# Two adjacent weight rows per partition, and the small start-up vectors on two queues, in a one-core encoder block with 32 experts

## The chip, the core and the metric

The kernel runs on one core of one Trainium2 chip. The core has five engines that run their own instruction streams: TensorE (PE; its weight loads are shown apart as PEld), VectorE (DVE), ScalarE (ACT), GpSimd (POOL) and SyncE (SP). Data comes from the chip's main memory by DMA, on 16 DMA engines that work for the core. A DMA is issued by an instruction of SP's or ACT's stream, in the order of that stream; in the profile such issues stand under SPq and ACTq, and the packets of SP's queue under q1, those of ACT's under q10.

The metric is the device time of one execution in microseconds (us). Before the change it is 1523.5 us, the median of 3 runs (1523.36 to 1524.43). The execution that was profiled took 1525.76 us, and the span of its trace, from the first to the last instruction, is 1524.1 us.

## The reference, cut to what matters

One layer over 256 tokens of width 1024: a mixer (attention and a state-space scan), a cross-attention, and a mixture of experts. The experts are where the changed loads feed in:

```python
logits = (xt @ w_router) + b_router                  # 256 tokens, 32 experts
top_vals, top_idx = lax.top_k(logits, TOP_K)         # 4 of 32
probs = jax.nn.softmax(top_vals, axis=-1)
...
def expert_block(args):
    xb, e = args
    g = jnp.minimum(xb @ w_e_gate[e] + b_e_gate[e], SWIGLU_LIMIT)
    u = jnp.clip(xb @ w_e_up[e] + b_e_up[e], -SWIGLU_LIMIT, SWIGLU_LIMIT)
    act = (u + 1.0) * g * jax.nn.sigmoid(SWIGLU_ALPHA * g)
    return act @ w_e_down[e] + b_e_down[e]
```

Each expert has three float32 matrices of 1024 x 1024 (4 MB each). All 32 experts are run, so 384 MB of weights pass through the core. The five vectors that change queue are the gain and bias of the first layer norm (`ln_in_g`, `ln_in_b`) and three of the scan: `dt_bias` and `a_log` (32 numbers each, for a softplus and a decay) and `d_skip` (32 numbers, one per scan head, that scale a skip path).

## The kernel before, in words

**Start.** The input `x` is fetched on SP's queue in four pieces, then `ln_in_g` and `ln_in_b` into rows of the tile `rows_a`, then the first five entries of a plan of weight blocks (`W.preload(5)`, L82: the first 1 MB in two halves, then two of 1 MB), then the other small vectors in rows (L225). The input is normalised (L270), transposed on TensorE (L278), scaled by the layer norm's gain and bias on ScalarE (L284), and split on VectorE into two parts `hTh` and `hTl` (L48, L49). Every weight block is also split into `w_h` (ScalarE, L96) and `w_l` (VectorE, L97), and a projection is three products (L237, L239, L240). Blocks come into three buffers `w_raw`; a scheduler orders each engine's stream by its own estimate of times.

**The scan's vectors.** `d_skip` is laid out by two DMAs (L392) as `dcol`: 64 partitions each read the same 16 numbers with a step of two. `dt_bias` and `a_log` follow on the same queue (L394, L395) into the two columns of `dtb`, one number per partition. ScalarE makes `nega` from `a_log` (L397), and VectorE changes its sign (L398).

**The mixture of experts.** A ring of 21 buffers `mw` of 1 MB takes the expert matrices in chunks of 256 rows (`fetch`, L662): partition p of a chunk holds row p and row 128 + p. A buffer is filled again when TensorE has read it. The plan takes the experts in pairs: gate and up of both (16 chunks), then down of both (8 chunks). Four experts make a quad; at its start `gather` (L961) selects each expert's at most 64 tokens with a product of the normalised input `xh`, `xl` (the weight load) and a selection matrix, and scales the result by `ln2_g` and `ln2_b` per feature (L966, L968). A chunk is used by 8 recorded matmuls (L935): the activations are loaded as weights, and the chunk streams by. Between up and down the activations are transposed (L948). `scatter` (L981) adds the results to the tokens. Experts with more than 64 tokens have a loop of their own (L1064 on) with its own loads (L1101); the trace shows no load of it. The down matrix of the last expert comes in pieces of 256 columns (L659), so that the first half of the output can be finished early.

Of the kernel before, what the change touches and what calls it, by code (L numbers as in the profile page):

```python
# [6 lines left out]
F32 = mybir.dt.float32  # L7
# [111 lines left out]
def body(nc, tc, a, out, dbg=None, stop=99):  # L119
# [7 lines left out]
    with es:  # L127
# [30 lines left out]
        for key, rows in (("a", ROWS_A), ("b", ROWS_B)):  # L158
            rowt[key] = (cst if key == "a" else xt_p).tile([P, P], F32, name="rows_" + key)
            n = 0  # L160
            for name, k in rows:
                if name.startswith("ln_in"):
                    nc.sync.dma_start(rowt[key][n:n + k], flat(name))
                else:
                    rest.append((rowt[key][n:n + k], flat(name)))
                at[name] = (key, n)
                n += k

# [51 lines left out]
                plan_block(a["w_xo"][0], "xo", 512 * i)  # L220

        plan_all()
        W.preload(5)
        for t, v in rest[::-1]:
            nc.sync.dma_start(t, v)  # L225

        def proj_t(name, c0, kts, xh, xl, r0=0):
# [141 lines left out]
        with tc.tile_pool(name="st", bufs=1, reuse_waits="tile") as st_p:  # L369
# [16 lines left out]
            nc.gpsimd.memset(past, 0.0)  # L386
            nc.gpsimd.affine_select(past, past, pattern=[[1, P]], compare_op=ALU.is_ge, fill=NEG, base=0,
                                    channel_multiplier=-1)
            dcol = xt_p.tile([P, 16], F32, name="dcol")
            dsv = a["d_skip"][0].rearrange("(c t) -> t c", t=2)  # L390
            for t in range(2):
                nc.sync.dma_start(dcol[64 * t:64 * t + 64], dsv[t:t + 1].broadcast_to([64, 16]))  # L392
            dtb = xt_p.tile([32, 2], F32, name="dtb")
            nc.sync.dma_start(dtb[:, 0:1], a["dt_bias"][0].rearrange("(p o) -> p o", o=1))  # L394
            nc.sync.dma_start(dtb[:, 1:2], a["a_log"][0].rearrange("(p o) -> p o", o=1))  # L395
            nega = xt_p.tile([32, 1], F32, name="nega")
            nc.scalar.activation(nega, dtb[:, 1:2], AF.Exp)  # L397
            nc.vector.tensor_scalar(nega, nega, -1.0, None, op0=ALU.mult)  # L398
# [247 lines left out]
        def fetch(upto):  # L646

            if not looped[0]:
                upto = min(upto, len(plan) // 2 + nslots - 4)
            while len(got) < min(upto, len(plan)):  # L650
                w, e, c = plan[len(got)]
                t = slot()
                if w == 2 and e == NE - 1:

                    t = t.rearrange("p j (k i f) -> p (j k) i f", k=2, i=2)
                    v = wes[w][e].rearrange("(c k p) (j i f) -> c p k j i f", c=2, p=P, j=2, i=2)[c % 2, :, :, :, c // 2]
                    for k in (slice(0, 2), slice(2, 4)) if c == 3 else (slice(0, 4),):
                        for i in range(2):
                            nc.sync.dma_start(t[:, k, i], v[:, k, i])  # L659
                    got.append(t)  # L660
                    continue
                ins = nc.sync.dma_start(t, wes[w][e, 256 * c:256 * c + 256].rearrange("(k p) f -> p k f", p=P))  # L662
                if len(ring) < nslots:
                    tc.keep_in_program_order(ins)
                got.append(t)
# [50 lines left out]
        nc.gpsimd.iota(iop_i, pattern=[[0, 1]], base=0, channel_multiplier=1)  # L716
        iop = cst.tile([P, 1], F32, name="iop")
        nc.gpsimd.tensor_copy(iop, iop_i)
        oneb = cst.tile([P, 1], BF16, name="oneb")
        nc.gpsimd.memset(oneb, 1.0)  # L720
        upb = cst.tile([P, P], BF16, name="upb")
# [217 lines left out]
        def swiglu(pg, gt, ut, st):  # L939
# [3 lines left out]
            nc.vector.scalar_tensor_tensor(ut, ut, 1.0, gt, op0=ALU.add, op1=ALU.mult)  # L943
            nc.vector.tensor_tensor(ut, ut, st, op=ALU.mult)

        def act_t(ut, pa, aT):
            for f in range(4):
                nc.tensor.transpose(pa[:, P * f:P * f + P], ut[:, P * f:P * f + P], ident)  # L948
            nc.scalar.activation(aT, pa.rearrange("p (f i c) -> p f i c", f=4, i=2), AF.Copy)  # L949

        def gather(sel, xg, n, ps, kts=(0, KT)):

            w = 512 // n
            for kt in range(*kts, w):
                p = ps()
                for i in range(w):
                    o = p[:, n * i:n * i + n]
                    for x in (xh, xl):
                        for b in range(NB):
                            s = slice(P * (kt + i), P * (kt + i) + P)  # L960
                            nc.tensor.matmul(o, x[:, b, s], sel[:, b], start=i == 0 and b == 0 and x is xh,  # L961
                                             stop=b == NB - 1 and x is xl, skip_group_check=True)
                for i in range(w):
                    o, g, b_ = p[:, n * i:n * i + n], col("ln2_g", kt + i), col("ln2_b", kt + i)
# [73 lines left out]
        def overflow():  # L1038
# [25 lines left out]
            with tc.If(nv > 0), tc.For_i(0, nv, 1):  # L1064
# [29 lines left out]
                for w in range(3):  # L1094
# [3 lines left out]
                    for c in range(4):  # L1098
                        wt = wb[n % 3]
                        n += 1  # L1100
                        nc.sync.dma_start(wt, wes[w][bass.ds(ev, 1), 256 * c:256 * c + 256].rearrange(  # L1101
                            "o (k p) f -> p (o k) f", p=P))
# [239 lines left out]
```

## Time and profile before

| | |
|---|---|
| median of 3 runs | 1523.5 us |
| the profiled execution | 1525.76 us |
| its span | 1524.1 us |
| PE busy | 1397.0 us (92%) |
| DVE, ACT busy | 635.6 us (42%), 415.7 us (27%) |
| moved by DMA | 489.69 MB, mean 321 GB/s |
| granted TensorE clock | 0.978 of full speed |

Busy time of PE has to be read with care: matmuls overlap, their ends are modelled, and a matmul that waits for its data inside the pipeline looks busy. The slices of the span tell more than the shares: the DMA engines are about half busy in the first third of the span and full from a bit past it to the end.

### The profile page before, as it was taken

Reading aid. Unit: us, or ns where it says so; the run is one execution under the profiler, and the core shown is the slowest. Engines: PE = TensorE matmul, PEld = TensorE weight load, DVE = VectorE, ACT = ScalarE, POOL = GpSimd, SP = SyncE. Lnnn points to the kernel's source line nnn. Section 1 sums busy time; section 2 is a strip of 40 time slices with the busy share of each in tenths; the row PEclk is TensorE's granted clock in tenths of the full one; section 3 lists DMA queues with packets and bytes.
Section 4 is the critical chain, followed back from the end, with each engine's and each line's share of the span. In section 5 each row is a group of like instructions: output and inputs, shape, how many; then the busy total and the mean of one; then the engine's idle time right before and its main releaser. Section 6 shows DMA issues by size and latency. Waiting matters only on the chain. (4 is left out here: it accounts for less than half of the span.)

```text
span 1524.1 us, 19108 instructions
## 1 busy us (share of the span) xinstructions
PE 1397.0 (92%) x7884; PEld 800.6 (53%) x7884; DVE 635.6 (42%) x1001; ACT 415.7 (27%) x656; POOL 19.2 (1%) x36
## 2 busy tenths in 40 slices
PE   2899999999999999989999999979889899888996
PEld 2898899998999863333333333324224233223233
DVE  3756568889877652441222121222112212212123
ACT  2557578687555411010010010001001001001010
POOL 1000000000000010000000000000000000000001
PEclk8899999999999999999999999989999999999999
DMA  3654536454595789999999999999999999999996
GB/s 113 183 169 162 181 124 209 152 194 139 192 327 173 252 302 398 409 409 404 409 409 409 409 409 409 409 409 355 409 409 409 409 410 409 409 409 408 409 409 235
DMA packets 154109, 489.69 MB, mean 321 GB/s; under 512 B 12396, under 2 KB 16996, under 8 KB 154020
## 3 DMA queue, kind: packets, MB, share of 16 engines
q1 hardware_dynamic: 153876, 488.18, 83.8%
q8 instruction: 63, 1.03, 0.3%
q10 hardware_dynamic: 144, 0.26, 0.0%
q14 instruction: 26, 0.21, 0.0%
HBM read 487.33 MB, written 1.08 MB: 320 GB/s over the span
## 5 line engine op out<-in xcount | busy, mean ns | idle before, releaser
L935 PE MATMUL ps_gu<-mw,xg 128*64 128x512 f32 x2048 | 465.8, 596 | 6.2 <-DMA mw<-in_w_e_up 3.8
L935 PEld LDWEIGHTS ps_gu<-mw,xg 128*64 128x64 f32 x2048 | 145.8, 137 | 280.4 <-issue 250.2
L935 PE MATMUL ps_y<-mw,aT 128*64 128x512 f32 x992 | 228.8, 599 | 14.7 <-DMA mw<-in_w_e_down 14.7
L97 DVE TENSOR_TENSOR w_l<-w_raw,w_h 128x1024 fp32r<-128x1024 f32 x145 | 175.8, 1217 | 90.1 <-ACT w_h L96 89.0
L96 ACT ACTIVATE w_h<-w_raw 128x1024 fp32r<-128x1024 f32 x145 | 152.6, 1055 | 122.7 <-PE ps_t L239 72.6
L239 PE MATMUL ps_t<-hTl,w_h 128*128 128x256 f32 x576 | 165.4, 288 | 21.4 <-DVE hTl L49 21.4
L237 PE MATMUL ps_t<-hTh,w_h 128*128 128x256 f32 x576 | 165.2, 288 | 2.0 <-DVE gx L327 2.0
L240 PE MATMUL ps_t<-hTh,w_l 128*128 128x256 f32 x576 | 164.0, 287 | 0.0
L935 PEld LDWEIGHTS ps_y<-mw,aT 128*64 128x64 f32 x992 | 70.9, 137 | 155.3 <-issue 124.3
L239 PEld LDWEIGHTS ps_t<-hTl,w_h 128*128 128x128 f32 x576 | 110.9, 193 | 21.8 <-DVE hTl L49 21.6
L237 PEld LDWEIGHTS ps_t<-hTh,w_h 128*128 128x128 f32 x576 | 110.8, 193 | 2.8 <-issue 2.8
L240 PEld LDWEIGHTS ps_t<-hTh,w_l 128*128 128x128 f32 x576 | 110.2, 192 | 0.4 <-issue 0.4
L942 DVE TENSOR_SCALAR ut<-ps_gu 128x512 f32<-128x512 f32 x32 | 22.1, 692 | 207.3 <-PE ps_gu L935 207.2
L949 ACT ACTIVATE aT<-ps_x 128x512 f32<-128x512 f32 x32 | 19.1, 597 | 314.5 <-PE ps_x L948 314.5
L889 PE MATMUL ps_gu<-bgu,ident 128*64 128x512 f32 x256 | 70.7, 619 | 28.4 <-DVE ut L942 13.5
L976 DVE SCALAR_TENSOR_TENSOR y<-ps_y,scl,y 128x512 fp32r<-128x512 f32 x30 | 22.5, 751 | 173.5 <-ACT y L975 167.6
L940 DVE TENSOR_SCALAR gt<-ps_gu 128x512 f32<-128x512 f32 x32 | 22.1, 691 | 159.3 <-PE ps_gu L935 159.3
L975 ACT ACTIVATE y<-ps_y,scl 128x512 fp32r<-128x512 f32 x30 | 19.0, 684 | 242.1 <-PE ps_y L935 197.5
L941 ACT ACTIVATE st<-gt 128x512 f32<-128x512 f32 x32 | 20.1, 629 | 198.2 <-DVE gt L940 198.2
L889 PEld LDWEIGHTS ps_gu<-bgu,ident 128*64 128x64 f32 x256 | 16.9, 138 | 72.2 <-DVE ut L942 29.4
L983 DVE TENSOR_TENSOR h<-h,ps_x 128x512 f32<-128x512 f32 x60 | 38.8, 682 | 15.2 <-PE ps_x L982 15.2
L968 ACT ACTIVATE xg<-ps_x,cols_a 128x256 f32<-128x256 f32 x32 | 18.1, 565 | 94.4 <-PE ps_x L961 94.4
(348 smaller groups left out, 1793.4 us busy)
## 6 DMA issues: line engine op xcount, KB each, us to landing
mw<-in_w_e_gate SPq DMA_DIRECT2D x128, 1024.0 KB
mw<-in_w_e_up SPq DMA_DIRECT2D x128, 1024.0 KB
mw<-in_w_e_down SPq DMA_DIRECT2D x124, 1024.0 KB
w_raw<-in_w_in SPq DMA_DIRECT2D x39, 1024.0 KB
w_raw<-in_w_ssd SPq DMA_DIRECT2D x8, 1024.0 KB
w_raw<-in_w_sb SPq DMA_DIRECT2D x4, 1024.0 KB
csb<-csd SPq DMA_DIRECT2D x8, 512.0 KB
w_raw<-in_w_mix_out SPq DMA_DIRECT2D x4, 1024.0 KB
```

The lines of the kernel that those rows point to most:

```text
L96: nc.scalar.activation(h, src, AF.Copy)
L97: nc.vector.tensor_tensor(l, src, h.bitcast(F32), op=ALU.subtract)
L237: nc.tensor.matmul(o, wh[:, k, s], xh[:, kt], start=first and j % 2 == 0, stop=False, skip_group_check=True)
L239: nc.tensor.matmul(o, wh[:, k, s], xl[:, kt], start=False, stop=False, skip_group_check=True)
L240: nc.tensor.matmul(o, wl[:, k, s], xh[:, kt], start=False, stop=last, skip_group_check=True)
L889: nc.tensor.matmul(pg[w][64 * i:64 * i + 64], hot4(2 * w + i), bgu, start=True, stop=False, skip_group_check=True)
L935: nc.tensor.matmul(dst[i], lhs(2 * c + k), chunk[:, k, 512 * i:512 * i + 512], start=first and c == 0 and k == 0, stop=c == 3 and k == 1, ...
L940: nc.vector.tensor_scalar(gt, pg[0], LIMIT, None, op0=ALU.min)
L941: nc.scalar.activation(st, gt, AF.Sigmoid, scale=1.702)
L942: nc.vector.tensor_scalar(ut, pg[1], -LIMIT, LIMIT, op0=ALU.max, op1=ALU.min)
L976: nc.vector.scalar_tensor_tensor(yl[r], y2[i][r], scl[r, i:i + 1], yh[r].bitcast(F32), op0=ALU.mult, op1=ALU.subtract)
L983: nc.vector.tensor_tensor(h2[:, b, s], h2[:, b, s], ps, op=ALU.add)
```

## The change

Two things change. First, partition p of an expert's chunk takes rows 2p and 2p + 1 of the 256 instead of rows p and 128 + p. The two are adjacent in memory, so each partition reads one run of 8 KB instead of two runs of 4 KB. What TensorE contracts must follow: feature 256 c + 2p + k now stands in partition p of slice k. So `gather` and the transposes of the activations read their columns with a step of two (`pairs`), and the per-feature scale and bias of `gather` come from a small table `gb2` in that order. The last expert's down matrix is cut in 16 pieces of 256 KB instead of 10 pieces.

Second, `ln_in_g`, `ln_in_b`, `dt_bias`, `a_log` and `d_skip` are issued from ScalarE's stream, ahead of its first computation; `d_skip` comes as one row of 32 numbers and is spread over the partitions by a matmul with a row of minus ones. The other vectors stay on SP's queue behind the first weights.

```diff
-                if name.startswith("ln_in"):
-                    nc.sync.dma_start(rowt[key][n:n + k], flat(name))
-                else:
-                    rest.append((rowt[key][n:n + k], flat(name)))
+                rest.append((rowt[key][n:n + k], flat(name)))
...
+        dtb = xt_p.tile([32, 2], F32, name="dtb")
+        drow = xt_p.tile([1, NHEAD], F32, name="drow")
+        for t, v in (*rest[:2], (dtb[:, 0:1], a["dt_bias"][0].rearrange("(p o) -> p o", o=1)),
+                     (dtb[:, 1:2], a["a_log"][0].rearrange("(p o) -> p o", o=1)),
+                     (drow, a["d_skip"][0].rearrange("(o e) -> o e", o=1))):
+            nc.scalar.dma_start(t, v)
         W.preload(5)
-        for t, v in rest[::-1]:
+        for t, v in rest[:1:-1]:
             nc.sync.dma_start(t, v)
...
+            ps = px.tile([P, 512], F32, tag="x", name="ps_ds")
+            nc.tensor.matmul(ps[:, :NHEAD], nones[0:1], drow, start=True, stop=True)
             for t in range(2):
-                nc.sync.dma_start(dcol[64 * t:64 * t + 64], dsv[t:t + 1].broadcast_to([64, 16]))
...
+                r = slice(64 * t, 64 * t + 64)
+                nc.vector.tensor_scalar(dcol[r], ps[r, t:NHEAD:2], -1.0, None, op0=ALU.mult)
...
-                    for k in (slice(0, 2), slice(2, 4)) if c == 3 else (slice(0, 4),):
+                    for g in range(2):
                         for i in range(2):
-                            nc.sync.dma_start(t[:, k, i], v[:, k, i])
+                            nc.sync.dma_start(t[:, 2 * g:2 * g + 2, i], v[g, :, :, i])
...
-                ins = nc.sync.dma_start(t, wes[w][e, 256 * c:256 * c + 256].rearrange("(k p) f -> p k f", p=P))
+                ins = nc.sync.dma_start(t, wes[w][e, 256 * c:256 * c + 256].rearrange("(p k) f -> p k f", p=P))
...
+        rows2 = xt_p.tile([8, 256], F32, name="rows2")
+        for j, n in enumerate(("ln2_g", "ln2_b")):
+            nc.sync.dma_start(rows2[4 * j:4 * j + 4], a[n][0].rearrange("(c f) -> c f", f=256))
+        gb2 = cst.tile([P, 2, 8], F32, name="gb2")
+        ps = px.tile([P, 512], F32, tag="x", name="ps_gb2")
+        for k in range(2):
+            nc.tensor.transpose(ps[:, 8 * k:8 * k + 8], rows2[:, k:256:2], ident[:8, :8])
+        nc.vector.tensor_copy(gb2, ps[:, :16].rearrange("p (k j) -> p k j", k=2))
...
+        def pairs(kt):
+
+            return slice(256 * (kt // 2) + kt % 2, 256 * (kt // 2) + 256, 2)
+
         def act_t(ut, pa, aT):
             for f in range(4):
-                nc.tensor.transpose(pa[:, P * f:P * f + P], ut[:, P * f:P * f + P], ident)
+                nc.tensor.transpose(pa[:, P * f:P * f + P], ut[:, pairs(f)], ident)
...
-                            s = slice(P * (kt + i), P * (kt + i) + P)
-                            nc.tensor.matmul(o, x[:, b, s], sel[:, b], start=i == 0 and b == 0 and x is xh,
+                            nc.tensor.matmul(o, x[:, b, pairs(kt + i)], sel[:, b], start=i == 0 and b == 0 and x is xh,
```

The order of the instructions moves at three places that matter below. At the start of ScalarE's stream, before the change (`w_h` is the rounded half of a weight block, `ln_t` the scaled input, `nega` the decay made from `a_log`):

```order
L133 ACT_TABLE_LOAD
L96 ACTIVATE w_h<-w_raw 128x1024 x2
L284 ACTIVATE ln_t<-ps_tr,cols_a 128x256 x4
L96 ACTIVATE w_h<-w_raw 128x1024 x2
L284 ACTIVATE ln_t<-ps_tr,cols_a 128x256 x4
L397 ACTIVATE nega<-dtb 32x1
L96 ACTIVATE w_h<-w_raw 128x1024 x3
```

And with the change:

```order
L133 ACT_TABLE_LOAD
L226 DMA rows_a<-in_ln_in_g 8x128
L226 DMA rows_a<-in_ln_in_b 8x128
L226 DMA dtb<-in_dt_bias 32x1
L226 DMA dtb<-in_a_log 32x1
L226 DMA drow<-in_d_skip 1x32
L401 ACTIVATE nega<-dtb 32x1
L96 ACTIVATE w_h<-w_raw 128x1024 x2
L288 ACTIVATE ln_t<-ps_tr,cols_a 128x256 x4
```

The five issues and `nega` now stand ahead of ScalarE's first weight split, where `nega` stood behind four splits and eight scalings.

On SP's queue behind the small rows, before the change (`bgu` holds the experts' biases, `wr` the router's weights, `w_raw 128x8x32` the columns of the projection for dt):

```order
L225 DMA rows_a<-in_ln_g 8x128
L392 DMA dcol<-in_d_skip 64x16x1 x2
L394 DMA dtb<-in_dt_bias 32x1
L395 DMA dtb<-in_a_log 32x1
L82 DMA w_raw<-in_w_in 128x4x512
L706 DMA bgu<-in_b_e_gate 32x512 x2
L706 DMA bgu<-in_b_e_up 32x512 x2
L73 DMA w_raw<-in_w_in 128x8x32
L709 DMA wr<-in_w_router 128x8x32
L82 DMA w_raw<-in_w_in 128x4x512 x7
```

And with the change:

```order
L229 DMA rows_a<-in_ln_g 8x128
L82 DMA w_raw<-in_w_in 128x4x512
L712 DMA bgu<-in_b_e_gate 32x512 x2
L712 DMA bgu<-in_b_e_up 32x512 x2
L715 DMA wr<-in_w_router 128x8x32
L728 DMA rows_4645<-in_ln_g 4x256
L728 DMA rows_4645<-in_ln_b 4x256
L73 DMA w_raw<-in_w_in 128x8x32
L82 DMA w_raw<-in_w_in 128x4x512 x7
```

The four DMAs of `dcol` and `dtb` are gone from between the small rows and the sixth weight DMA; `wr` and the two rows for `gb2` go ahead of the dt columns.

Where the expert chunks are issued in rows, at the start of the mixture of experts on SP's queue, before the change:

```order
L662 DMA mw<-in_w_e_gate 128x2x1024 x4
L662 DMA mw<-in_w_e_up 128x2x1024 x4
L662 DMA mw<-in_w_e_down 128x2x1024 x5
L1150 DMA bdn<-in_b_e_down 32x512 x2
L662 DMA mw<-in_w_e_down 128x2x1024 x3
```

And with the change:

```order
L668 DMA mw<-in_w_e_gate 128x2048 x4
L668 DMA mw<-in_w_e_up 128x2048 x4
L668 DMA mw<-in_w_e_down 128x2048 x5
L1169 DMA bdn<-in_b_e_down 32x512 x2
L668 DMA mw<-in_w_e_down 128x2048 x3
```

The number and the order of the chunks stay; each is now one run of 2048 numbers per partition instead of two of 1024.

## Rows read from the trace of the kernel before

**Rows 1.** The profile page: the span, and in 40 equal slices of it the busy share of the DMA engines in tenths and what they moved.

```profile
span 1524.1 us, 19108 instructions
...
DMA  3654536454595789999999999999999999999996
GB/s 113 183 169 162 181 124 209 152 194 139 192 327 173 252 302 398 409 409 404 409 409 409 409 409 409 409 409 355 409 409 409 409 410 409 409 409 408 409 409 235
```

**Rows 2.** Busy time in stretches of the mixture of experts. Columns: the stretch in us from the span's start, its length, busy us (and instructions) of PE, PEld, DVE, ACT, POOL, then the granted TensorE clock, the busy share of the DMA engines, and GB/s.

```profile
600.00:640.00 40.00, 40.00 (x186) 14.20 (x184) 10.33 (x27) 0.95 (x2) 0.00 (x0) 1.00 1.03 409
1040.00:1080.00 40.00, 38.76 (x188) 14.27 (x184) 7.71 (x14) 2.45 (x4) 0.00 (x0) 1.00 0.91 356
564.00:1494.00 930.00, 856.59 (x3970) 312.38 (x3970) 224.97 (x409) 79.36 (x131) 0.00 (x0) 0.99 1.02 405
```

**Rows 3.** Who waited for whom over the whole span: total us, times, longest. The rows in which TensorE or its weight load waits for an expert's down matrix.

```profile
PEld ps_y L935 <- DMA mw<-in_w_e_down: 28.9, 22, 2.4
PE ps_y L935 <- DMA mw<-in_w_e_down: 14.7, 20, 3.3
```

**Rows 4.** The chain of work that ended last, in order of time: start, us, what. Its first and its last stretch of DMA.

```profile
1066.95 19.05 DMA mw<-in_w_e_down
...
1448.06 18.46 DMA mw<-in_w_e_up
```

**Rows 5.** TensorE's instructions in order of time at the start of five quads (quads 0, 1, 2, 6 and 7), where the gather begins: start, us, what.

```profile
558.63 0.70 PE L961 MATMUL ps_x<-sel,xh 128*128 128x256 f32 x2
...
681.39 0.51 PE L961 MATMUL ps_x<-sel,xh 128*128 128x256 f32 x2 [0.25 <-DVE h L983]
...
793.12 0.79 PE L961 MATMUL ps_x<-sel,xh 128*128 128x256 f32 x2
...
1267.26 0.79 PE L961 MATMUL ps_x<-sel,xh 128*128 128x256 f32 x2
...
1391.22 0.50 PE L961 MATMUL ps_x<-sel,xh 128*128 128x256 f32 x2 [0.26 <-DVE h L983]
```

**Rows 6.** DMA by size: from the page the packets of the whole span and the issues of the gate matrices (count, KB each); then two stretches, columns as in rows 2, in which the queue is full of runs of 2 KB (`w_raw`, 512 columns) and of 1 KB (the last expert's pieces of 256 columns).

```profile
DMA packets 154109, 489.69 MB, mean 321 GB/s; under 512 B 12396, under 2 KB 16996, under 8 KB 154020
...
mw<-in_w_e_gate SPq DMA_DIRECT2D x128, 1024.0 KB
...
12.00:13.50 1.50, 0.24 (x1) 0.25 (x2) 1.36 (x3) 1.50 (x4) 0.00 (x0) 1.00 1.06 392
1498.00:1503.00 5.00, 5.00 (x26) 1.78 (x26) 0.00 (x0) 0.00 (x0) 0.00 (x0) 1.00 1.10 349
```

**Rows 7.** SP's DMA issues from 17 to 40 us: start, us until the last of them was issued, what.

```profile
17.75 1.43 SPq L392 DMA_DIRECT2D dcol<-in_d_skip  x2
19.23 3.11 SPq L394 DMA_DIRECT2D dtb<-in_dt_bias  x1
22.38 0.42 SPq L395 DMA_DIRECT2D dtb<-in_a_log  x1
22.92 0.39 SPq L82 DMA_DIRECT2D w_raw<-in_w_in  x1
```

**Rows 8.** Instructions in order of time at 42 us, with the idle time of the engine before them and what ended it.

```profile
41.96 0.20 ACT L397 ACTIVATE nega<-dtb 32x1 f32<-32x1 f32 x1 [24.12 <-DMA dtb<-in_a_log]
...
42.26 1.27 DVE L49 TENSOR_TENSOR hTl<-ln_t,hTh 128x512 fp32r<-128x512 f32 x2
...
42.99 0.58 PE L239 MATMUL ps_t<-hTl,w_h 128*128 128x256 f32 x1 [21.43 <-DVE hTl L49]
```

**Rows 9.** Busy time in stretches around that wait, columns as in rows 2.

```profile
22.00:24.00 2.00, 0.00 (x0) 0.00 (x0) 0.00 (x0) 0.00 (x0) 0.00 (x0) 1.00 0.05 0
30.00:32.00 2.00, 0.00 (x0) 0.00 (x0) 0.00 (x0) 0.00 (x0) 0.00 (x0) 0.50 0.05 0
43.00:46.50 3.50, 3.50 (x16) 3.50 (x17) 2.80 (x3) 1.06 (x2) 0.00 (x0) 0.50 0.64 119
46.50:50.00 3.50, 3.50 (x30) 3.50 (x29) 1.22 (x1) 1.12 (x2) 0.00 (x0) 0.93 0.87 280
```

**Rows 10.** The first ten microseconds, in order of time, as in rows 7 and 8; the last row is the one DMA that ScalarE's queue issues before the change (x count: least, median and most ns).

```profile
0.80 1.28 ACT L133 ACT_TABLE_LOAD   x1 [0.80 <-PEq L1331]
...
3.08 0.28 SPq L163 DMA_DIRECT2D rows_a<-in_ln_in_b  x1
...
7.25 0.26 PE L173 MATMUL ps_prm<-ident,rows_a 16*128 16x16 f32 x1 [7.25 <-DMA rows_a<-in_ln_in_b]
...
8.11 1.70 DVE L270 TENSOR_SCALAR h<-h,ln_mv,ln_rs 128x1024 f32<-128x1024 f32 x2
...
9.87 1.06 ACT L96 ACTIVATE w_h<-w_raw 128x1024 fp32r<-128x1024 f32 x1 [7.79 <-DMA w_raw<-in_w_in]
...
L1302 ACTq DMA_DIRECT2D out<-h x1: 372/372/372, 1519.5 to 1519.5; - x1
```

**Rows 11.** Instructions grouped by line, shapes kept apart: count, busy us, mean ns of one, and idle time before them. The gather's matmul and weight load, and the weight load of the activations' transposes.

```profile
L961 PE MATMUL ps_x<-sel,xh 128*128 128x256 f32 x128 | 30.6, 323 | 0.7 <-DVE h L983 0.7
L961 PEld LDWEIGHTS ps_x<-sel,xh 128*128 128x128 f32 x128 | 21.7, 209 | 18.6 <-DVE xg L966 8.9 <-issue 5.7 <-DVE h L983 3.9
L948 PEld LDWEIGHTS ps_x<-ident,ut 128*128 128x128 f32 x128 | 13.4, 140 | 30.2 <-issue 20.3 <-DVE ut L944 8.3 <-DVE gt L940 1.6
```

**Rows 12.** SP's issues of the last expert's down matrix: start, us until the last was issued, count.

```profile
1481.19 21.62 SPq L659 DMA_DIRECT2D mw<-in_w_e_down  x10
```

More of the change, by code (lines that the diff above doesn't have):

```diff
@@ L389, in body @@
             dcol = xt_p.tile([P, 16], F32, name="dcol")
-            dsv = a["d_skip"][0].rearrange("(c t) -> t c", t=2)
+            ps = px.tile([P, 512], F32, tag="x", name="ps_ds")
+            nc.tensor.matmul(ps[:, :NHEAD], nones[0:1], drow, start=True, stop=True)
             for t in range(2):
-                nc.sync.dma_start(dcol[64 * t:64 * t + 64], dsv[t:t + 1].broadcast_to([64, 16]))
-            dtb = xt_p.tile([32, 2], F32, name="dtb")
-            nc.sync.dma_start(dtb[:, 0:1], a["dt_bias"][0].rearrange("(p o) -> p o", o=1))
-            nc.sync.dma_start(dtb[:, 1:2], a["a_log"][0].rearrange("(p o) -> p o", o=1))
+                r = slice(64 * t, 64 * t + 64)
+                nc.vector.tensor_scalar(dcol[r], ps[r, t:NHEAD:2], -1.0, None, op0=ALU.mult)
             nega = xt_p.tile([32, 1], F32, name="nega")
@@ L655, in fetch @@
                     t = t.rearrange("p j (k i f) -> p (j k) i f", k=2, i=2)
-                    v = wes[w][e].rearrange("(c k p) (j i f) -> c p k j i f", c=2, p=P, j=2, i=2)[c % 2, :, :, :, c // 2]
-                    for k in (slice(0, 2), slice(2, 4)) if c == 3 else (slice(0, 4),):
+                    v = wes[w][e].rearrange("(c g p k) (j i f) -> c g p k j i f", c=2, g=2, p=P, j=2,
+                                            i=2)[c % 2, :, :, :, :, c // 2]
+                    for g in range(2):
                         for i in range(2):
-                            nc.sync.dma_start(t[:, k, i], v[:, k, i])
+                            nc.sync.dma_start(t[:, 2 * g:2 * g + 2, i], v[g, :, :, i])
                     got.append(t)
                     continue
-                ins = nc.sync.dma_start(t, wes[w][e, 256 * c:256 * c + 256].rearrange("(k p) f -> p k f", p=P))
+                ins = nc.sync.dma_start(t, wes[w][e, 256 * c:256 * c + 256].rearrange("(p k) f -> p k f", p=P))
                 if len(ring) < nslots:
@@ L959, in gather @@
                         for b in range(NB):
-                            s = slice(P * (kt + i), P * (kt + i) + P)
-                            nc.tensor.matmul(o, x[:, b, s], sel[:, b], start=i == 0 and b == 0 and x is xh,
+                            nc.tensor.matmul(o, x[:, b, pairs(kt + i)], sel[:, b], start=i == 0 and b == 0 and x is xh,
                                              stop=b == NB - 1 and x is xl, skip_group_check=True)
                 for i in range(w):
-                    o, g, b_ = p[:, n * i:n * i + n], col("ln2_g", kt + i), col("ln2_b", kt + i)
+                    o, g, b_ = p[:, n * i:n * i + n], *[gb2[:, (kt + i) % 2, 4 * j + (kt + i) // 2:4 * j + (kt + i) // 2 + 1]
+                                                        for j in range(2)]
                     if i % 2:
@@ L1101, in overflow @@
                         nc.sync.dma_start(wt, wes[w][bass.ds(ev, 1), 256 * c:256 * c + 256].rearrange(
-                            "o (k p) f -> p (o k) f", p=P))
+                            "o (p k) f -> p (o k) f", p=P))
                         lhs = (lambda kt: aT[:, kt % 4, kt // 4]) if w == 2 else (lambda kt: xg[:, kt, 0:CAP])
```

## The prediction, made before the change was run

> **What bounds the kernel now.** I read the slices of the page first. From the sixteenth slice on the DMA engines are full and move 409 GB/s; before that they are about half busy [rows 1]. So the span has two parts with different limits. In the first, some 560 us, TensorE's products set the pace; in the second, the experts' 384 MB.
>
> The table of stretches says how firm the second limit is: 409 GB/s at a share of 1.03 from 600 to 640 us, and 405 GB/s on the mean of the 930 us from 564 to 1494, one dip to 356 included [rows 2]. TensorE looks busy there too, but a matmul that waits inside the pipeline looks busy. The waits name the down matrices as what its weight loads wait for, 28.9 us in 22 waits, beside 14.7 us of its matmuls [rows 3], and in the chain of what ended last stretches of DMA begin at 1066.95 us and the last of 18.46 us begins at 1448.06 [rows 4]. The starts of the quads show why only from there: quad 1 lasts 793.12 - 681.39 = 111.7 us with a full ring behind it, quad 6 lasts 1391.22 - 1267.26 = 124.0 us [rows 5]. A quad's 48 chunks of 1.0486 MB need 123.1 us at 409 GB/s. TensorE alone is 11 us quicker per quad than the loads, uses up the ring's stock by about 1060 us, and then runs at the pace of the loads.
>
> The first part has one large hole. At 21.6 us TensorE stops for 21.4 us: it waits for `hTl`, VectorE's `hTl` stands behind the sign change of `nega`, and ScalarE's `nega` stands 24.1 us until `a_log` has landed [rows 8]. `a_log` was issued at 22.38, behind the two DMAs of `dcol` and that of `dt_bias` [rows 7]. In the hole the DMA engines are 0.05 busy and move nothing that shows [rows 9]: 0.05 is a little under one engine of 16. The two `dcol` DMAs ask for 2 x 64 x 16 = 2048 numbers of 4 bytes; some 20 us for them would be about 10 ns each on one engine (an estimate from these rows).
>
> **The change, part by part.** The sum is made against the profiled execution: 1525.8 us, a span of 1524.1 and 1.7 around it, 2.3 us above the median.
>
> *The start.* `dcol`'s DMAs are gone, and `dt_bias` and `a_log` are issued some 19 us earlier on another queue. The hole of 21.4 us goes: -21.4. With it goes a slow restart: from 43 to 46.5 us the granted clock is 0.50 (1.2 GHz, after the idle time) and 16 matmuls start, in the next 3.5 us 30 do [rows 9]; the 16 would have taken 16/30 of 3.5 us = 1.9, so -1.6.
>
> What could be late next are the weights. When TensorE reached 21.6 us it had used two of the six half-blocks of the first 3 MB. Four are left, of 24 matmuls each at 3.5/30 = 0.117 us [rows 9]: 11 us, to about 33 us. The next weight DMA was issued at 22.92 [rows 7]; with four DMAs gone from ahead of it, it can go at about 17.75. Its 1.05 MB take 2.7 us at 392 GB/s [rows 6], and a small DMA behind loads took 4.2 us to arrive (issued 3.08, used 7.25) [rows 10]: in hand by about 25 us, 8 us early.
>
> What the new order adds is a wait ahead of everything on ScalarE and VectorE: `nega` now stands before ScalarE's first weight split (9.87 us) and its sign change before VectorE's normalisation (8.11 us) [rows 10]; behind them queue the splits, `hTh`, `hTl` and TensorE. ScalarE is done with its table load at 2.08; an issue on its queue took 0.37 us [rows 10], so `a_log`, the fourth, is issued at about 3.6 and, with the same 4.2 us, is there at 7.8: cost 0 to 0.3 us. If the issue of `dt_bias` takes 3.11 us as on SP's queue [rows 7], it is 2.7 us later. The far end is that `a_log` arrives only after all of `x` and the first weights, about 14.5 us: 6.4 us late. I take +1.0, the nearest row being that of `ln_in_b`; in it are the few small additions to TensorE and VectorE (the product that spreads `d_skip`, two small transposes, three copies), each like the 0.26 us transpose of rows 10. Start: -22.0, from -16 to -23. Everything behind shifts with it, since the ring and the stream start when the first part ends.
>
> *The stream.* Each partition's two runs of 4 KB become one of 8 KB. No load of 8 KB runs is in the trace, so it is bounded by the shorter ones. With the queue full the rates are 349 GB/s for 1 KB, 392 for 2 KB, 409 for 4 KB [rows 2, 6]; per engine (16 of them) that is 46.9, 83.6 and 160.2 ns a run. A fixed part and a part per KB, through 1 and 4 KB: 9.2 + 37.8 per KB, so 8 KB take 311.4 ns, 421 GB/s. Through 2 and 4 KB: 7.0 + 38.3, 313.4 ns, 418 GB/s. I take 419, by the nearer pair. The lower end is no gain (runs cut at 4 KB on the way, or 409 a limit of something else), the upper one no fixed part at all, 16 x 1024/37.8 = 433 GB/s. The stretch of 930 us moved 405 x 930 = 376.7 MB [rows 2]: 921 us at 409, 899 at 419, so -22.
>
> The Trainium skill, DMA: Bandwidth & Descriptors, section Why small descriptors are slow (HBM only), gives a fixed overhead of about 3 cycles per packet of 32-byte beats. By it 8 KB would save 3 beats in some 260, 1.2% or about 11 us, and the sum would be near 1491; but from 2 to 4 KB it would give 2.3%, where rows 6 and 2 show 4.3%.
>
> Can TensorE follow? At 419 a quad's load takes 120.1 us, still over its own 111.7, so the loads stay what ends last from about quad 1 on. In quad 0 TensorE itself needs 681.39 - 558.63 = 122.8 us [rows 5]; the ring is full there and a faster load waits for free buffers, so the 2.7 us of that quad are not had. Stream: -19. If loads cost nothing, TensorE's own 111.7 us would bring quad 7 to 681.4 + 6 x 111.7 = 1351.6, against 1391.2: some 40 us is the most.
>
> *Columns with a step of two.* The gather's and the transposes' weight loads now read every second number. A quad has 32 + 16 of them (256 and 128 in 8 quads [rows 11]). No weight load with a step is in the trace. From below they cost 0; from above, the whole 0.209 us of a gather's load once more [rows 11], 10 us a quad. I take 0: that load runs beside a matmul of 0.323 us, and TensorE has 8 us a quad to spare. Without that cover it is the third rival.
>
> *The end.* The last expert's matrix has 16 issues instead of 10, 6 x 0.3 us more on SP, inside 21.6 us in which SP waits for buffers [rows 12]: 0. The runs there stay 1 KB.
>
> Sum: 1525.8 - 21.4 - 1.6 + 1.0 - 19 = 1484.8 for an execution like the profiled one; less 2.3, **1482** as a median.
>
> **The rivals.** *The rate stays 409.* For it: 409 holds to a unit in nearly every slice, as a ceiling would. Against it: the steps from 1 to 2 to 4 KB have not flattened to nothing. Then only the start counts: 1525.8 - 22 - 2.3 = 1501.5.
>
> *The vectors come no sooner.* `a_log` shares the DMA engines with 1 MB of `x` and 3 MB of weights, lands near 14.5 us, and holds ScalarE and VectorE from the start. 6.4 us late instead of 1.0: 1488. Against it: `ln_in_b`, behind all of `x` on one queue, was there at 7.25 [rows 10]. The Trainium skill, same page, section Issuing engines are not separate DMA queues, says that a second issuing engine saves issue time only, since all run on the same DMA engines; that speaks for this rival.
>
> *Slower: the stepped weight loads are paid in full.* TensorE then needs 121.7 us a quad and becomes the limit. Quad 0 starts at 536.6 and takes 132.8, six quads 730.2, so quad 7 starts at 1399.6; from there to the end the span before took 132.9 with about 12 of waits, now 131: 1530.5, +1.7 - 2.3 = 1530, slower by 0.4%. It decides from 0.19 us per load: with x us a quad, 536.6 + 122.8 + 6 x 111.7 + 120.9 + 8x reaches 1524.1 at x = 9.2. For it: 48 such loads a quad sit on the engine that is next in line. Against it: they run beside matmuls.
>
> *Both ends good.* No fixed part per run, 433 GB/s: 118 us a quad even so, 921 - 870 = -51 cut by TensorE's 40 us: 1525.8 - 22 - 40 - 2.3 = 1461.
>
> **How the numbers follow.** Forecast 0.62; rate unchanged 0.18; vectors no sooner 0.08; both ends good 0.07; slower 0.05. The forecast alone, with 414 to 424 GB/s and the start's bounds, spans 1473 to 1495. Rival one and a start of -20 set the upper end at 1504; the lower one, 1467, takes in part of the last rival. About 0.2% (3 us) is what a measurement here can tell from no change. Every case but the third rival lies over 15 us below 1523.5; a milder form of it gives no change. Faster 0.93, same 0.02, slower 0.05.
>
> **What would show it.** The hole at 21 to 43 us gone and TensorE running through with the granted clock at 1.00; `nega` near 8 us; the first quad's gather near 537 us; packets of 8 KB, half as many, and slices of about 419 GB/s; quads of 120 us late and 112 early; the gather's matmuls still 0.32 us. I am wrong if the slices stay at 409, if TensorE's early quads take over 115 us, or if ScalarE's first split begins after 11 us.

## The result, and the profile after the change

The changed kernel takes 1483.9 us (median of 4 runs, 1478.9 to 1484.2), the kernel before 1523.6 (4 runs, 1523.4 to 1524.4). The ratio is 0.9731, with a 95% interval of 0.971 to 0.9752: some 40 us less. The profiled execution took 1483.58 us, its span is 1481.9.

The page of the changed kernel, the lines that answer to [rows 1, 6], and the shares of the chain that ended last:

```profile
span 1481.9 us, 19128 instructions
...
DMA  7545345543685789999999999999999999999995
GB/s 244 171 163 179 124 162 171 199 153 132 254 298 177 284 316 421 420 393 413 418 420 420 419 420 420 419 419 373 419 419 420 420 419 420 419 419 419 420 420 202
DMA packets 103503, 489.69 MB, mean 330 GB/s; under 512 B 10422, under 2 KB 15030, under 8 KB 54774
...
DMA 20%; PE 11%; DVE 1%; issue 0%; ACT 0%; DVEq 0%; SPq 0%
...
mw<-in_w_e_gate SPq DMA_DIRECT2D x128, 1024.0 KB, 19.9
```

The full slices stand at 419 to 420 GB/s where 409 stood. The first slice moves 244 GB/s instead of 113. 103503 - 54774 = 48729 packets have 8 KB or more; 89 had before.

The start, in order of time as in [rows 7, 8, 10]:

```profile
0.83 0.60 ACTq L226 DMA_DIRECT2D rows_a<-in_ln_in_g  x1
...
2.13 0.44 ACTq L226 DMA_DIRECT2D dtb<-in_a_log  x1
...
3.95 0.26 PE L170 MATMUL ps_prm<-ident,rows_a 16*128 16x16 f32 x1 [3.95 <-DMA rows_a<-in_ln_in_b]
...
5.96 0.20 ACT L401 ACTIVATE nega<-dtb 32x1 f32<-32x1 f32 x1 [3.88 <-DMA dtb<-in_a_log]
...
9.11 1.06 ACT L96 ACTIVATE w_h<-w_raw 128x1024 fp32r<-128x1024 f32 x1 [2.94 <-DMA w_raw<-in_w_in]
...
17.05 0.39 SPq L82 DMA_DIRECT2D w_raw<-in_w_in  x1
```

`nega` runs at 5.96 us instead of 41.96, the first weight split at 9.11 instead of 9.87, and the sixth weight DMA is issued at 17.05 instead of 22.92. Stretches, columns as in [rows 2]: the first 40 us, and two of the stream.

```profile
0.00:40.00 40.00, 29.98 (x226) 28.82 (x227) 28.22 (x52) 21.79 (x32) 3.80 (x20) 1.00 0.73 230
600.00:640.00 40.00, 37.76 (x164) 12.82 (x162) 24.82 (x54) 3.01 (x5) 0.00 (x0) 1.00 1.01 420
1040.00:1080.00 40.00, 37.58 (x176) 12.85 (x174) 8.92 (x16) 2.50 (x4) 0.00 (x0) 1.00 1.01 419
```

TensorE starts 226 recorded matmuls in the first 40 us with the clock granted in full; the hole is gone. The starts of the same quads as in [rows 5], and of quad 4:

```profile
535.10 0.80 PE L979 MATMUL ps_x<-sel,xh 128*128 128x256 f32 x2
...
658.03 0.52 PE L979 MATMUL ps_x<-sel,xh 128*128 128x256 f32 x2 [0.25 <-DVE h L1002]
...
769.74 0.51 PE L979 MATMUL ps_x<-sel,xh 128*128 128x256 f32 x2 [0.25 <-DVE h L1002]
...
1006.62 0.63 PE L979 MATMUL ps_x<-sel,xh 128*128 128x256 f32 x3
...
1229.85 0.80 PE L979 MATMUL ps_x<-sel,xh 128*128 128x256 f32 x2
...
1349.20 0.52 PE L979 MATMUL ps_x<-sel,xh 128*128 128x256 f32 x2 [0.24 <-DVE h L1002]
```

Quad 4 of the kernel before starts here:

```profile
1028.56 0.62 PE L961 MATMUL ps_x<-sel,xh 128*128 128x256 f32 x3
```

Against the kernel before that is 23.5 us earlier at quad 0, 23.4 at quads 1 and 2, 21.9 at quad 4, 37.4 at quad 6, 42.0 at quad 7, and 42.2 at the end of the span. So the start gave 23.5 us, the first four quads nothing (1.6 us were lost again), and the stream the other 18.7, all of it from quad 4 on. There TensorE waited for transfers before and hardly does now. Its waits for DMA from the start of quad 4 to the start of quad 7 (total us, times, longest), before and after:

```profile
PE ps_y L935 <- DMA mw<-in_w_e_down: 13.5, 18, 3.3
...
PE ps_gu L935 <- DMA mw<-in_w_e_up: 3.2, 6, 0.6
...
PE ps_gu L935 <- DMA mw<-in_w_e_gate: 2.2, 4, 0.9
```

```profile
PE ps_y L950 <- DMA mw<-in_w_e_down: 1.6, 3, 0.6
PE ps_gu L950 <- DMA mw<-in_w_e_up: 0.8, 2, 0.6
```

Groups by line and shape as in [rows 11], and what of [rows 3] is left, with the largest wait of SP's queue (total us, times, longest):

```profile
L979 PE MATMUL ps_x<-sel,xh 128*128 128x256 f32 x128 | 30.9, 326 | 0.7 <-DVE h L1002 0.7
L979 PEld LDWEIGHTS ps_x<-sel,xh 128*128 128x128 f32 x128 | 22.4, 217 | 18.8 <-DVE xg L985 9.7 <-issue 5.1 <-DVE h L1002 4.0
L967 PEld LDWEIGHTS ps_x<-ident,ut 128*128 128x128 f32 x128 | 17.7, 207 | 30.2 <-issue 20.3 <-DVE ut L959 8.3 <-DVE gt L955 1.6
```

```profile
PEld ps_y L950 <- DMA mw<-in_w_e_down: 5.9, 6, 1.4
PE ps_y L950 <- DMA mw<-in_w_e_down: 1.6, 3, 0.6
SPq L668 <- DMA mw<-in_w_e_gate: 195.4, 95, 2.3
```

With a step of two the gather's load takes 217 ns for 209 and its matmul 326 for 323 (means); the transposes' load takes 207 for 140. Of the 28.9 and 14.7 us of waits for the down matrix 5.9 and 1.6 are left.

### The profile page after: what moved, and what is told of

It reads as the page before. It is cut to its first block, busy times and chain, and to the rows that moved or that the text cites. A ratio compares the mean times of both kernels' runs of the same rounds, so it can differ in the third digit from the quotient of the medians.

```text
span 1481.9 us, 19128 instructions
## 1 busy us (share of the span) xinstructions
PE 1391.4 (94%) x7888; PEld 802.9 (54%) x7888; DVE 635.1 (43%) x1004; ACT 416.4 (28%) x656; POOL 16.8 (1%) x36
## 2 busy tenths in 40 slices
DMA packets 103503, 489.69 MB, mean 330 GB/s; under 512 B 10422, under 2 KB 15030, under 8 KB 54774
## 5 line engine op out<-in xcount | busy, mean ns | idle before, releaser
L950 PE MATMUL ps_y<-mw,aT 128*64 128x512 f32 x992 | 225.4, 597 | 1.7 <-DMA mw<-in_w_e_down 1.6
L904 PE MATMUL ps_gu<-bgu,ident 128*64 128x512 f32 x256 | 72.0, 630 | 28.9 <-DVE ut L957 13.5
L987 ACT ACTIVATE xg<-ps_x,gb 128x256 f32<-128x256 f32 x32 | 18.1, 564 | 94.4 <-PE ps_x L979 94.4
```

The costliest lines, as they stand in the source:

```text
L904: nc.tensor.matmul(pg[w][64 * i:64 * i + 64], hot4(2 * w + i), bgu, start=True, stop=False, skip_group_check=True)
L950: nc.tensor.matmul(dst[i], lhs(2 * c + k), chunk[:, k, 512 * i:512 * i + 512], start=first and c == 0 and k == 0, stop=c == 3 and k == 1, ...
```

## The experiments

**The two halves of the change, each alone.** The first run has only what concerns the vectors, the second only what concerns the rows (with the stepped columns and `gb2`):

```diff
+            nc.scalar.dma_start(t, v)
         W.preload(5)
-        for t, v in rest[::-1]:
+        for t, v in rest[:1:-1]:
```

```diff
-                ins = nc.sync.dma_start(t, wes[w][e, 256 * c:256 * c + 256].rearrange("(k p) f -> p k f", p=P))
+                ins = nc.sync.dma_start(t, wes[w][e, 256 * c:256 * c + 256].rearrange("(p k) f -> p k f", p=P))
```

> The kernel before with the start of the changed one alone (five vectors on ScalarE's queue, d_skip as a row); the expert chunks stay in two runs of 4 KB. Theory (the two gains are separate and add): the hole of 21.4 us at 21 us is gone, the first gather comes near 535 us as in the changed kernel, the stream stays at 409 GB/s, time about 1500 us (1498 to 1502). Rival (the earlier start also speeds the stream up, so that the parts don't add): slices above 412 GB/s and below 1495 us.

> The changed kernel with the start of the one before: 8 KB runs alone. Theory: the hole stays, the first gather is at about 558 us, slices at 419 GB/s, time about 1505 us (1503 to 1507), and the two parts add up to the whole 40 us. Rival (the stream gains because it starts earlier): 409 GB/s and 1520 us or more.

The start alone took 1500.3 us (1499.5 to 1503.1; ratio 0.9848, 0.9829 to 0.9868): its slices stand at 409 and its first gather starts at 532.6 us. The rows alone took 1505.6 (1504.7 to 1506.3; ratio 0.9875, 0.9858 to 0.9892): its slices stand at 419 to 420, and the hole is there as before:

```profile
41.56 0.20 ACT L399 ACTIVATE nega<-dtb 32x1 f32<-32x1 f32 x1 [23.78 <-DMA dtb<-in_a_log]
...
42.59 0.58 PE L240 MATMUL ps_t<-hTl,w_h 128*128 128x256 f32 x1 [20.04 <-DVE hTl L49]
```

The kernel before, run beside them, took 1524.9 us (1521.9 to 1526.3). The halves save 24.6 and 19.3 us, 43.9 together, where the whole saved 39.7. That is as near as runs that differ by up to 5 us among themselves can show: the two halves are separate, each has its own effect in the trace, and they add up to the whole within the scatter.

**What held the queue.** Two runs split the start. In one all vectors stay on SP's queue, and only the layout of `d_skip` changes; in the other `dt_bias` and `a_log` go to ScalarE's queue, and the two DMAs of `dcol` stay:

```diff
+            nc.sync.dma_start(drow, a["d_skip"][0].rearrange("(o e) -> o e", o=1))
...
-                nc.sync.dma_start(dcol[64 * t:64 * t + 64], dsv[t:t + 1].broadcast_to([64, 16]))
```

```diff
+        for t, v in ((dtb[:, 0:1], a["dt_bias"][0].rearrange("(p o) -> p o", o=1)),
+                     (dtb[:, 1:2], a["a_log"][0].rearrange("(p o) -> p o", o=1))):
+            nc.scalar.dma_start(t, v)
```

> The kernel before, with d_skip as one row of 128 bytes on SP's queue in the place of its two spread DMAs; dt_bias and a_log stay on SP's queue behind it, nothing goes to ScalarE's queue. Theory (the 2048 pieces of 4 bytes hold the queue): the hole shrinks to under 4 us, time 1500 to 1504 us. Rival (the queue decides: a_log is late because it is issued late behind the small rows on SP): the hole stays over 10 us, 1512 us or more.

> The kernel before with dt_bias and a_log on ScalarE's queue at the start; the two spread DMAs of d_skip stay on SP's queue. Theory (the pieces of 4 bytes hold what is queued behind them, here the sixth weight DMA): nega comes near 6 us and TensorE runs on at 21 us, but runs dry near 33 us and waits some 8 to 12 us for weights that land near 42 us; time 1509 to 1515 us. Rival (only a_log's place matters): no hole, 1500 us.

The first took 1501.7 us, inside the 1499.5 to 1503.1 of the start alone: `a_log`, issued at 17.78 on the old queue, let `nega` run at 19.48, and TensorE's longest wait from 10 to 60 us is 1.4 us. The second took 1515.4 us. `nega` ran at 4.32, but the weights behind `dcol` were late (a timeline of it around 44 us):

```profile
43.40 1.06 ACT L96 ACTIVATE w_h<-w_raw 128x1024 fp32r<-128x1024 f32 x1 [21.65 <-DMA w_raw<-in_w_in]
...
44.51 0.58 PE L241 MATMUL ps_t<-hTh,w_h 128*128 128x256 f32 x1 [12.23 <-ACT w_h L96]
```

And the DMA engines were as idle as in [rows 9]:

```profile
30.00:32.00 2.00, 2.00 (x20) 2.00 (x18) 0.00 (x0) 0.00 (x0) 0.00 (x0) 1.00 0.05 0
```

So the cause is the two DMAs that lay out `dcol`, which hold everything behind them for some 20 us. The trace of the kernel before shows their pieces: from 20 to 32 us the queue carries packets of 4 bytes alone, 319 to 328 in each 3 us, one in 9.1 to 9.4 ns. Which queue the vectors use makes no difference that shows once those two are gone. Without that layout the hole of 21.4 us goes; with it TensorE still stops for 12.2 us, for weights, even when `a_log` is issued ahead of it on the other queue. Whether the size of the pieces, their number or the step between them makes that layout slow was not tried apart.

**Is it the length of a run or the order of addresses?** Both runs keep two adjacent rows per partition. One takes them in two DMAs of one row each (4 KB a run), the other in two DMAs of half of both rows (2 KB a run):

```diff
+                for k in range(2):
+                    ins = nc.sync.dma_start(t[:, k], v[:, k])
```

```diff
+                for i in range(2):
+                    s = slice(512 * i, 512 * i + 512)
+                    ins = nc.sync.dma_start(t[:, :, s], v[:, :, s])
```

> The changed kernel, same two adjacent rows per partition, but each chunk in two DMAs of one row per partition: runs of 4 KB, taken from every second row. Theory (the length of a run decides): slices back at 409 GB/s, time 1500 to 1504 us. Rival (the order of the addresses decides, adjacent rows per partition): 419 GB/s and 1482 to 1486 us.

> The changed kernel, same rows per partition, but each chunk in two DMAs of half the columns: runs of 2 KB. Theory (a fixed part per run of 7 to 9 ns): 392 GB/s as for the 2 KB runs of the first part, the stream of 376.7 MB takes 961 us instead of 899, quads of 128 us once the stock is used up, time 1535 to 1548 us. Rival (only runs over 4 KB differ): 409 GB/s, about 1502 us.

The first took 1504.7 us, 0.7 above the expected range, at 409 GB/s; the length decides. That a chunk now comes in two DMAs is not the reason: the kernel before has one DMA a chunk and the same 409. The second took 1558.2, 10 us more than the top of what was expected. Its stretch from 600 to 640 us:

```profile
600.00:640.00 40.00, 37.76 (x164) 12.86 (x162) 24.83 (x54) 3.01 (x5) 0.00 (x0) 1.00 1.05 386
```

The 392 GB/s of [rows 6], from which the expectation came, were read over 1.5 us; over 40 us runs of 2 KB give 386.

**Longer runs.** Four adjacent rows per partition, 16 KB a run, in 10 buffers of 2 MB instead of 21 of 1 MB; the gather and the transposes step by four:

```diff
-MR = 7, 7, 3, 4
+MR = 3, 4, 1, 2
...
+                ins = nc.sync.dma_start(t, wes[w][e, 512 * c:512 * c + 512].rearrange("(p k) f -> p k f", p=P))
...
+            return slice(512 * (kt // 4) + kt % 4, 512 * (kt // 4) + 512, 4)
```

> Four adjacent rows per partition: chunks of 512 rows in 10 buffers of 2 MB, runs of 16 KB, gather and transposes with a step of four, same computation. Theory (fixed part per run): 16 KB take 614 to 620 ns per engine, 423 to 427 GB/s; the stream gains 8 to 17 us more, less what coarser buffers cost TensorE (up to 5 us): 1470 to 1482 us. Rival (419 GB/s is a ceiling of another kind): slices stay at 419 to 420 and the time is 1484 us or more.

It took 1498.3 us (ratio 0.9824, 0.9807 to 0.984), a plain miss: the loads reached the theory's rate, but the time is the rival's, slower than the changed kernel. Its stretch from 700 to 820 us, and its gather (count: least, median and most ns):

```profile
700.00:820.00 120.00, 112.49 (x514) 43.01 (x512) 28.32 (x49) 9.70 (x16) 0.00 (x0) 1.00 1.01 427
```

```profile
L981 PE MATMUL ps_x<-sel,xh x128: 348/397/602, 535.3 to 1371.9; 128*128 128x256 f32 x128
...
L981 PEld LDWEIGHTS ps_x<-sel,xh x128: 307/329/334, 535.3 to 1371.7; 128*128 128x128 f32 x128
```

In the changed kernel the same view has 284 and 198 ns, in the kernel before 280 and 188. A step of four costs what a step of two did not: 113 ns a matmul, 32 of them a quad, 3.6 us.

**Wide steps by themselves.** The changed kernel with its 8 KB runs, its gather stepping by eight and its transposes by four:

```diff
-                nc.tensor.transpose(pa[:, P * f:P * f + P], ut[:, pairs(f)], ident)
+                nc.tensor.transpose(pa[:, P * f:P * f + P], ut[:, f:512:4], ident)
-                            nc.tensor.matmul(o, x[:, b, pairs(kt + i)], sel[:, b], start=i == 0 and b == 0 and x is xh,
+                            nc.tensor.matmul(o, x[:, b, kt + i:D:8], sel[:, b], start=i == 0 and b == 0 and x is xh,
```

> The changed kernel with a step of eight in the gather's columns and of four in those of the activations' transposes, instead of two; the weights stay in their order, so it computes products of other features with these weights. Theory (weight loads with a step run beside the matmuls): the gather's matmuls stay under 0.35 us, quad 1 lasts 111 to 113 us, time 1482 to 1487 us. Rival (loads with a wide step are paid in full, 0.2 us each): quad 1 lasts 120 us or more and the time is over 1500 us.

1506.6 us (one run): the rival's time, 23 us slower than the changed kernel at the same 420 GB/s, and matmuls of 404 ns where the theory had under 350. Quad 1 lasts 113.9 us, though, near the theory's 111 to 113 and not the rival's 120: the loss is spread over the quads.

```profile
L979 PEld LDWEIGHTS ps_x<-sel,xh x128: 312/337/343, 535.1 to 1379.0; 128*128 128x128 f32 x128
L979 PE MATMUL ps_x<-sel,xh x128: 398/404/607, 535.2 to 1379.2; 128*128 128x256 f32 x128
```

The chain that ended last has no transfer in it any more (shares of the span, from its page):

```profile
PE 30%; DVE 2%; ACT 0%; issue 0%; DVEq 0%
```

A step of eight is hardly worse than one of four, so the price comes between two and four. The transposes' loads behave otherwise: a mean of 140 ns with no step, 207 with two, 210 with four.

**The steps taken out.** The copies `xh` and `xl` are written once in sorted columns, so that the gather reads adjacent ones; for 16 KB and for 8 KB runs (the latter with `k=2`):

```diff
-                split(nc, xh[:, b, s], xl[:, b, s], h2[:, b, s], copy=copy, sub=nc.gpsimd)
+                split(nc, *[x[:, b, s].rearrange("p (k q) -> p q k", k=4) for x in (xh, xl)],
+                      h2[:, b, s].rearrange("p (q k) -> p q k", k=4), copy=copy, sub=nc.gpsimd)
```

> The 16 KB version again, but its copies xh and xl of the normalised rows are written with their columns already sorted by row, so that the gather's weight loads read adjacent columns; nothing else differs. Theory (the run of the 16 KB version was lost to TensorE: its gather loads with a step of four elements took 329 ns instead of 198, a matmul every 397 ns instead of 284, 256 times 113 ns or 29 us, and no transfer stands in its last chain): loads return to 188 ns, matmuls to 280, the slices stay at 426 to 428 GB/s, the time falls under the changed kernel's: 1464 to 1476 us. Rival (ten buffers of 2 MB are too coarse, so that a matrix is waited for whole): the time stays at 1484 us or above with TensorE waiting for DMA or the stream below 420 GB/s, although the gather is back at 280 ns.

> The changed kernel with xh and xl written in sorted columns, so that the gather reads adjacent columns again; 8 KB runs and the transposes' step of two stay. Theory (a step of two elements costs 4 ns a gather matmul, about 1 us in 256, most of it behind the stream; the sorted write costs nothing that is waited for): 1482 to 1485 us, the same. Rival (the write of xh and xl with a step on VectorE, ScalarE and GpSimd holds up the first gather, or the step of two costs more than its durations say): first gather later than 537 us, or a time under 1479 us.

The first took 1479.6 us (1477.7 to 1482.8; ratio 0.971, 0.9688 to 0.9732): 18.7 us back, so the step was the cause of the miss, but 3.6 us above the top of what was expected. The second took 1481.0 (1478.8 to 1483.8; 0.9721, 0.9699 to 0.9744), between what the theory and the rival expected. Both intervals overlap that of the changed kernel; neither is shown to beat it. For the second that answers the question: a step of two costs nothing that shows, against a scatter of some 5 us.

What keeps the first from its gain is seen in two views: the shares of its chain that ended last, from its page, and the stretch from 640 to 680 us, in it and in the changed kernel:

```profile
PE 20%; DMA 10%; DVE 2%; ACT 0%; issue 0%; DVEq 0%; SPq 0%
```

```profile
640.00:680.00 40.00, 38.06 (x185) 16.53 (x183) 11.78 (x22) 4.75 (x8) 0.00 (x0) 1.00 0.87 356
```

```profile
640.00:680.00 40.00, 38.07 (x184) 16.41 (x182) 11.77 (x22) 4.75 (x8) 0.00 (x0) 1.00 0.95 388
```

TensorE and the transfers change places in that chain: the changed kernel has PE 11% and DMA 20%. With faster loads more of the end hangs on TensorE, which takes 112.8 us for each of quads 1 and 2 without a wait for a transfer. And from 640 to 680 us the loads move 356 GB/s against 388; that the larger buffers come free later there is a reading, and how much each of the two is worth was not tried apart.

**TensorE without the stream.** Half the bytes for the same work:

```diff
+                ins = nc.sync.dma_start(t[:, :, :512], wes[w][e, 256 * c:256 * c + 256, :512].rearrange("(p k) f -> p k f", p=P))
...
+                    nc.tensor.matmul(dst[i], lhs(2 * c + k), chunk[:, k, :512],
```

> The changed kernel fetches only the first 512 columns of each pair of rows of an expert (the last matrix and the looped part are untouched), and every matmul on them reads those columns twice, so that the second half of each product repeats the first: as much work for TensorE, half the bytes. Theory (at 419 GB/s the changed kernel is within some 20 us of what TensorE needs by itself, so that the 16 KB version with adjacent columns had little left to win): TensorE no longer waits for a transfer, the quads after the second take 109 to 113 us, and the time is 1458 to 1472 us. Rival (the stream is still the bound by a wide margin, and the 16 KB version was held up by something else, its coarse buffers): below 1445 us.

1445.2 us, below what the theory expected and at the rival's edge. It isn't a clean floor for the changed kernel: TensorE's instructions stand in another order from quad 1 on, since the scheduler reckons with smaller loads, and waits for VectorE go with it. The group of the bias products from 700 to 1300 us, in the changed kernel and in this one:

```profile
L904 PE MATMUL ps_gu<-bgu,ident 128*64 128x512 f32 x178 | 49.4, 640 | 23.5 <-DVE ut L957 10.3 <-DVE gt L955 7.1 <-PEq L1083 6.0
```

```profile
L904 PE MATMUL ps_gu<-bgu,ident 128*64 128x512 f32 x171 | 57.7, 618 | 3.4 <-PEq L1083 3.4
```

The 17.4 us of waits for VectorE are gone, but the group is busy for 8.3 us more. So the order is part of the reason why most of its quads last 109.5 us where the sorted 16 KB run takes 112.8; that it is all of it is not shown. What TensorE needs by itself in the changed kernel's order was not measured apart.

All runs in one table; the starts of the quads are read as above:

| run | us | first gather | quad 0 | mean of quads 1 to 6 | full slices, GB/s |
|---|---|---|---|---|---|
| before | 1523.6 | 558.6 | 122.8 | 118.3 | 409 |
| after | 1483.9 | 535.1 | 122.9 | 115.2 | 420 |
| start alone | 1500.3 | 532.6 | 122.8 | 118.2 | 409 |
| rows alone | 1505.6 | 557.0 | 122.5 | 115.3 | 420 |
| `d_skip` as a row, SP's queue | 1501.7 | 534.1 | 122.1 | 118.2 | 409 |
| `dcol` stays | 1515.4 | 549.0 | 123.0 | 118.1 | 409 |
| 4 KB runs | 1504.7 | 535.4 | 123.1 | 118.4 | 409 |
| 2 KB runs | 1558.2 | 534.3 | 123.1 | 126.6 | 386 |
| 16 KB, step 4 | 1498.3 | 535.3 | 124.8 | 116.9 | 427 |
| 8 KB, step 8 | 1506.6 | 535.2 | 129.0 | 117.4 | 420 |
| 16 KB, sorted | 1479.6 | 535.1 | 122.2 | 114.6 | 427 |
| 8 KB, sorted | 1481.0 | 533.1 | 122.3 | 115.1 | 420 |
| half the bytes | 1445.2 | 532.6 | 122.5 | 110.4 | not full |

## Why the prediction was right, point by point

1482 us was forecast, 1483.9 came, and each of the two large terms by itself was met.

**The start, -22.0; measured -23.5.** The hole and the slow restart went, as said, and so did the cause: `dcol`'s 4-byte pieces. The term "+1.0" for the new wait was off: it let ScalarE's issues begin after the table load at 2.08 us. They run beside it, from 0.83, `a_log` lands before 5.96, and ScalarE's first split comes 0.76 us sooner instead of later.

**The stream, -19; measured -18.7** (first gather to end: 965.5 us before, 946.8 after). The line through the shorter runs held: 419 was taken, 419 to 420 came. That it came so near is in part luck: the 392 GB/s for 2 KB was read over 1.5 us, and with the 386 of the 2 KB run the same pair gives 422. The 0.3 us between forecast and measurement is luck too, since executions differ by 5 us. That quad 0 would give nothing is right (122.9 for 122.8). But "the loads stay what ends last from about quad 1 on" is wrong: quads 1, 2 and 3 gave nothing either (111.7, 115.4 and 121.5 us for 111.7, 115.2 and 120.3), and the whole gain came in quads 4 to 6 (110.2, 113.0 and 119.3 for 120.6, 118.1 and 124.0). The chain that ended last in the changed kernel has its first stretch of DMA in quad 4, at about the time of the kernel before [rows 4]:

```profile
1061.65 20.05 DMA mw<-in_w_e_up
```

The sum came out even so: it counted on all quads but the first, and three of them gave it all. The 3-cycle rule of the Trainium skill (DMA: Bandwidth & Descriptors, Why small descriptors are slow (HBM only)), by which 1.2% was to come, gives too little here: 420 / 409 is 2.7%.

**The columns with a step of two, 0: right in size, wrong in its reason.** Loads and matmuls grew by 8 and 3 ns on the mean, 256 x 3 ns = 0.8 us in all. But the step said two more things. That the load runs beside its matmul is no cover for a wider step: at four the median load grew by 131 ns and the time of a matmul with it by 113. And "TensorE has 8 us a quad to spare" is a term that was mis-sized. It set a quad's load, 120.1 us, against the 111.7 of quad 1 alone, and took the loads to be what ends last from there on. But the ring is full of loaded chunks when the quads begin, and TensorE draws on them: in quads 1 to 5 of the changed kernel its matmuls wait for no transfer and its weight loads for 2.3 us in all, and these quads last 114.4 us on the mean. (Quad 3 is long for a reason of its own: TensorE waits 6.0 us once at L1083, the branch to the loop of the experts with more than 64 tokens, and the granted clock is 0.68 on the mean from 990 to 1006 us.) Up to the first transfer in the chain, at 1061.65 us, TensorE sets the pace, and nothing covers what is added to it. The run with a step of eight adds 120 ns x 32 = 3.8 us a quad, under half of those 8; it should have been free by that step, and it cost 23 us, 14.0 of them by the start of quad 4:

```profile
1020.62 0.75 PE L979 MATMUL ps_x<-sel,xh 128*128 128x256 f32 x2
```

Not all of it is the price of the loads. In quad 0 (129.0 us for 122.9) the first gather also waits 2.3 us for `xh`, of which it needs every column, and the granted clock from 537 to 541 us is 0.50, where the changed kernel has 0.83.

**The end, 0: right.** From the start of quad 7 to the end of the span 132.9 us before, 132.7 after.

**The rivals.** "The rate stays" fell with the rows alone, 420 GB/s. "The vectors come no sooner" fell with `nega` at 5.96. What the Trainium skill says (DMA: Bandwidth & Descriptors, Issuing engines are not separate DMA queues) holds all the same: with the 4-byte pieces gone, the second queue was worth nothing that shows, 1500.3 us with it and 1501.7 without. "Stepped loads paid in full" did not happen, but its mechanism is real one step further on; it was to decide from 0.19 us per load in 48 loads, 9.2 us a quad, and 3.6 us a quad was enough for 16 KB runs to lose more than they won. "Both ends good" was wrong in its rate: no 433 at 8 KB, and 427 at 16. (Its 118 us a quad is a slip, 48 chunks at 433 GB/s take 116.2; its sum went by the 40 us of TensorE and doesn't change.)

## What to carry to other kernels

Look at what stands ahead of a late DMA on its queue, and at the size of its pieces, before moving the late one: two DMAs with 2048 numbers of 4 bytes between them held a queue for some 20 us, and one row and a matmul replaced them. Where a stream is the limit, lengthen its runs, and read the gain from a line through the rates that the trace shows. But don't take the slack of the engine next in line from one quad. Look where the first transfer stands in the chain that ended last: as long as there is stock in the ring, here up to 1061 us, that engine sets the pace and has none. A rearrangement of the data that it must read with a wide step can then cost more than the longer runs win, and sorting the data once where it is written costs nothing that was seen here.

## What the runs showed of the hardware

- A run costs a fixed part and a part per KB, up to 16 KB (an estimate from the rates, the one for 1 KB read over 5 us only): with the queue full, 16 engines x bytes / rate gives 46.9 ns for 1 KB [rows 6], 84.9 for 2 (386 GB/s), 160.2 for 4 (409), 312 for 8 (420), 614 for 16 (427). From 8 to 16 KB that is still 37.7 ns per KB.
- A weight load of the gather (128 x 128) takes a median of 188 ns with adjacent columns of fp32, 198 with a step of two, 329 with four, 337 with eight. The Trainium skill (SBUF — State Buffer, Specifications (TRN2)) says that lines have 16 bytes and that a line wants two hits for full bandwidth: a step of two fp32 gives two, a step of four one. These four numbers agree with that; the transposes' loads, at means of 140, 207 and 210 ns for steps of one, two and four, do not show it.
- What SP's issues are said to wait for does not tell whether the stream is at its full rate. The largest wait was 280.5 us for TensorE in the kernel before, 195.4 for the gate matrices in the changed one, and 348.6 for TensorE in the sorted 16 KB run, and the full slices stood at 409, 420 and 427 GB/s. The slices and the chain that ended last tell it.
